# Output and down projections of a two-layer trunk with tokens as the stationary operand, and layer norms with tokens on partitions

## The chip, the cores and the metric

The kernel runs on one NeuronCore of a Trainium2 chip. The metric is the device time of one execution in microseconds, median of three runs. One execution is also profiled; its trace gives the start, duration and releaser of each instruction on TensorE (PE, with its weight loads as PEld), VectorE (DVE), ScalarE (ACT), GpSimd (POOL) and the DMA queues (SP's and ACT's among them).

## The reference

256 latent tokens `x` and 256 context tokens `ctx`, 1024 channels, pass through two layers. In layer 0 both go through all of it (512 tokens); in layer 1, the last, only the latent tokens go past the keys and values (256 tokens). All is float32. In each layer, for each stream:

```python
m = gates[..., 0, :] * attn_o + gates[..., 1, :] * conv_o + gates[..., 2, :] * pool_o
mix = m @ w_out + b_out                                          # 1024 x 1024
x = layer_norm(DEEPNORM_ALPHA * x + ml[..., 2, :] * mix, ln1_g[l], ln1_b[l])
h = modulate(x, ml[..., 3, :], ml[..., 4, :])                    # h*(1+scale)+shift
a, u = jnp.split(h @ w_up, 2, axis=-1)                           # 1024 x 5632
a = depthwise_conv(a, dw_w, dw_b)                                # 3 taps over tokens
f = (jax.nn.silu(a) * u) @ w_down                                # 2816 x 1024
x = layer_norm(DEEPNORM_ALPHA * x + ml[..., 5, :] * f, ln2_g[l], ln2_b[l])
```

`ml[..., i, :]` are six rows of 1024 numbers per layer and stream, made from a condition vector by `silu(c) @ w_ada + b_ada`. Rows 2 and 5 multiply (gate) the output and down projections.

## The kernel before

**Products.** Every fp32 matrix is held as a sum hi + lo of two fp32r parts, and a product is three passes, hi·hi, hi·lo, lo·hi (`mm3`, L389 to L395). Most products have a 128x128 piece of the weights as stationary operand and up to 512 tokens as moving operand, so the result in PSUM has channels on the partitions and tokens along the row. The q, k and v products are the other way round (`natural`): tokens stationary, 512 weight columns moving.

**Weights.** They come in as items in one fixed order (`ORDER`, made by `weight_order`). SP loads each item (`load_to`) eight items ahead, through a queue worked in order; ACT makes hi (L277), DVE makes lo by subtraction (L281), three items ahead (`split_to`), and `take` hands them out. Items named ada are products of their own for the condition rows (L329) that PE does at set places; adt and pre are side work. Activations, residuals and rows live in 55 slots of 512 floats per partition (`S`). PSUM has four buffers for products (`mmb`, names mm), three for transposes and attention (`aux`, names ax), one for ada.

**Output projection and norm 1 (L1027 to L1071).** The residual x of layer 0 is loaded by ACT's queue with channels on the partitions (L1017) and gets ALPHA and the gated bias on ACT (L1031). For each of eight 128-channel blocks, `mmB` makes the product, and `Residual.feed` evicts it on DVE (L511): product times gate, a number per channel, plus residual, into sT. In layer 0 the last four blocks are done for the two halves of the tokens (s = 0, 1) one after the other, with 256 tokens moving. After every second block `Norm.feed` transposes sT on PE (L460) to have tokens on partitions, ACT copies the result to nat (L462), and DVE takes its statistics (L467). `Norm.norm` works out mean and 1/sqrt(variance) (DVE, and a power on POOL, L475) and scales nat, on DVE (L488) and ACT (L484) by turns. `back` transposes nat back (L499), and `modulated` makes from it the input of the next products: hh on ACT (L531), h and hl on DVE (L533, L536), and xr, the residual times ALPHA and the norm's gain and offset, on ACT (L540).

**Up (L1077 to L1102).** Three up products begin by the k that are ready (`mm_by_k`). Each pair of products j is evicted by the three-tap conv, one ACT and two DVE operations (L1081, L1085, L1088), a silu on ACT and a product on DVE (L1093), and split into ah and al. A product waits until one of the four PSUM buffers is evicted.

**Down and norm 2 (L1104 to L1145).** As for the output projection, with 22 k-pieces per block in three weight items; in layer 0 the eighth block goes by halves. In layer 0 the norm leads to layer 1's first (conv) products, and the second half's norm is done later, among these. In layer 1 all products move 256 tokens, and the norm ends the kernel: gain and offset are applied on the back-transposed tiles, on ACT (L1141) and DVE (L1142), and four DMAs write the output, channels on the partitions.

**Order.** A scheduler places each engine's instructions; within an engine they run in that order. Splits (`pin`) keep the order in which they are written.

Of the kernel before, what the change touches and what calls it, by code (L numbers as in the profile page):

```python
# [13 lines left out]
P = 128  # L14
DEPTH = 2
# [24 lines left out]
NSLOT = 55  # L40
NFF = 3
# [7 lines left out]
GRP = 3  # L49
TAPS_LATER = 60  # L50
# [34 lines left out]
def weight_order(l):  # L85
# [57 lines left out]
def trunk(ctx: ExitStack, tc: tile.TileContext, xT, cT, crow, wst, vec, brow, grow, rope, icnt, ident, out):  # L143
# [140 lines left out]
    def take(it):  # L284

        while True:
# [4 lines left out]
            if ORDER[i][0] not in ("ada", "adt", "pre") and unfinished:  # L291
                unfinished.pop(0)()
# [7 lines left out]
    def take_ada():  # L300
# [10 lines left out]
        while unfinished:  # L311
            unfinished.pop(0)()
# [6 lines left out]
    ada_ps = {}  # L319
    unfinished = []  # L320
    due = []

    def ada(l, m, k):
        w = raw.pop(("ada", l, m, k))
        if k == 0:
            ada_ps[l, m] = pad.tile([P, 256], F32, tag="ad", name=uid("ad"))
        ps = ada_ps[l, m]
# [4 lines left out]
        if k == KT - 1:  # L332
            del ada_ps[l, m]
            row = sm(256, "adarow", bufs=1)
            V.tensor_copy(row, ps)
            unfinished.append(lambda: ada_end(l, m, row))
# [165 lines left out]
    class Residual:  # L502


        def __init__(self, gmod, xres, ns):
            self.ln, self.gmod, self.xres, self.ns, self.sT = Norm(), gmod, xres, ns, {}

        def feed(self, c, ps, s):
            if c not in self.sT:
                self.sT[c] = ST(self.ns * SEQ, name="sT")  # L510
            V.scalar_tensor_tensor(  # L511
                self.sT[c][:, half(s)], ps[:, half(s)], self.gmod[:, c, s:s + 1], self.xres[c][:, half(s)],
                op0=ALU.mult, op1=ALU.add,
            )
            if c % 2:
                self.ln.feed(c // 2, s, (self.sT[c - 1], self.sT[c]))

        def norm(self, s):
            self.ln.norm(s)

        def modulated(self, s, sA, sB, ag, ab, hs, xs, T, TX):

            for i in range(4):
                a = self.ln.back(i, s)
                for c2 in range(2):
# [11 lines left out]
                    if s * SEQ < TX:  # L537
                        if c not in xs:
                            xs[c] = ST(TX, name="xr")
                        A.activation(xs[c][:, half(s)], src, AF.Identity, scale=ag[:, c:c + 1], bias=ab[:, c:c + 1])  # L540

    def affine(l, name, shift, scale, tag):
# [7 lines left out]
        ag = const.tile([P, KT], F32, name=f"ag{tag}")  # L550
        ab = const.tile([P, KT], F32, name=f"ab{tag}")
        V.tensor_scalar(ag, col(l, name + "_g", 0, 8), ALPHA, None, op0=ALU.mult)
        V.tensor_scalar(ab, col(l, name + "_b", 0, 8), ALPHA, None, op0=ALU.mult)
        return sA, sB, ag, ab
# [93 lines left out]
    for l in range(DEPTH):  # L648
# [360 lines left out]
        if l == 0:  # L1009
            xres = []  # L1010
        its = [(take(("pw", l, c)), mmb()) for c in range(GRP)]
        mm_by_k(its, cT_, range(KT), T)
        for c in range(8):
            ps = its[c][1] if c < GRP else mmB(take(("pw", l, c)), cT_, T)
            if l == 0:
                xres.append(S(name="x"))
                A.dma_start(xres[c], xT[c])  # L1017
# [236 lines left out]
```

## Time and profile before

| | us |
|---|---|
| three runs | 1439.53, 1439.96, 1442.31 |
| median | 1439.96 |
| the profiled execution, its own time | 1439.88 |
| its span, first to last instruction | 1438.1 |

The span is what the trace covers. The execution's own time is 1.8 us longer. The granted clock of PE over the span was 0.993. In the rows of the profile a line with "xN" groups N instructions; the duration of a matmul reaches past the start of the next, since matmuls are pipelined, so what one costs in a stream is the distance from start to start. What stands in square brackets is the idle time ahead of an instruction and the instruction that ended it.

### The profile page before, as it was taken

How to read it: one execution, taken by the hardware profiler on the slowest of the kernel's cores; microseconds unless marked ns; L12 is line 12 of the kernel's file. 1: busy time of each engine (PE TensorE's matmuls, PEld its weight loads, DVE VectorE, ACT ScalarE, POOL GpSimd, SP SyncE). 2: the span in 40 equal slices, each digit the busy share in tenths (PEclk: the TensorE clock that was granted, in tenths of full speed). 3: DMA queues.
4: the chain of work that ended last, by engine and by line, in shares of the span. 5: the costliest groups of instructions: out<-in, count | busy, mean ns of one | idle time of the engine just before them, and what ended most of it. 6: DMA issues, size and time to landing. Idle time of an engine off the chain costs nothing.

```text
span 1438.1 us, 22130 instructions
## 1 busy us (share of the span) xinstructions
PE 1400.5 (97%) x8538; PEld 1207.9 (84%) x8538; DVE 1056.9 (73%) x1941; ACT 728.1 (51%) x1190; POOL 64.4 (4%) x59
## 2 busy tenths in 40 slices
PE   7999899999999999999999999899999999899997
PEld 5777678888877888888888888799889999799997
DVE  3598896996994747767666786379899967776653
ACT  3332346654737526554544321373687774655542
POOL 0020320000000000000000000001400000000000
PEclk9999999999999999999999999999999999999998
DMA  9654322223233415577765766878733355655540
GB/s 359 240 180 139 118 96 88 82 93 106 85 128 125 157 42 205 181 268 253 242 242 208 267 218 207 288 289 320 250 114 110 120 167 191 241 184 185 168 147 30
DMA packets 76649, 256.37 MB, mean 178 GB/s; under 512 B 8704, under 2 KB 9856, under 8 KB 76416
## 3 DMA queue, kind: packets, MB, share of 16 engines
q1 hardware_dynamic: 74416, 251.99, 50.5%
q10 hardware_dynamic: 2128, 2.96, 0.7%
q8 instruction: 67, 1.10, 0.3%
q14 instruction: 38, 0.31, 0.1%
HBM read 239.19 MB, written 15.73 MB: 177 GB/s over the span
## 4 chain that ended last, share of the span: by engine, by line
PE 73%; issue 20%; DVE 3%; ACT 2%; POOL 2%; DMA 1%; SPq 0%; POOLq 0%; ACTq 0%
PE mm L393 21%; PE mm L394 21%; PE mm L395 20%; PE ax L427 3%; PE ax L891 1%; PE ad L329 1%; PE ax L460 1%; PE ax L499 1%; POOL gc L721 1%; PE ax L393 1%; DVE lo L281 1%; PE ax L395 1%; PE ax L394 1%; PE ad L571 1%; DMA rt<-in_rope 1%
## 5 line engine op out<-in xcount | busy, mean ns | idle before, releaser
L277 ACT ACTIVATE hi<-raw 128x1024 fp32r<-128x1024 f32 (+2 forms) x212 | 218.5, 1038 | 281.5 <-PE mm L394 206.6
L393 PE MATMUL mm<-hh,hi 128*128 128x256 f32 (+1 forms) x1112 | 346.7, 317 | 8.1 <-ACT hh L531 4.6
L394 PE MATMUL mm<-hl,hi 128*128 128x256 f32 (+1 forms) x1112 | 350.3, 316 | 1.2 <-DVE hl L536 1.1
L395 PE MATMUL mm<-hh,lo 128*128 128x256 f32 (+1 forms) x1112 | 349.5, 316 | 0.0
L281 DVE TENSOR_TENSOR lo<-raw,hi 128x1024 fp32r<-128x1024 f32 (+1 forms) x193 | 229.9, 1194 | 100.6 <-ACT hi L277 96.7
L680 DVE SCALAR_TENSOR_TENSOR H<-gl,vt,H 128x502 f32<-128x502 f32 (+29 forms) x480 | 264.5, 606 | 0.1
L393 PEld LDWEIGHTS mm<-hh,hi 128*128 128x128 f32 x1112 | 209.5, 191 | 23.4 <-ACT hh L531 5.1
L394 PEld LDWEIGHTS mm<-hl,hi 128*128 128x128 f32 x1112 | 212.0, 191 | 16.8 <-DVE hl L536 2.3
L395 PEld LDWEIGHTS mm<-hh,lo 128*128 128x128 f32 x1112 | 212.1, 191 | 13.9 <-issue 1.1
L393 PE MATMUL mm<-hi,hi 128*128 128x512 f32 x464 | 186.1, 401 | 0.0
L395 PE MATMUL mm<-hi,lo 128*128 128x512 f32 x368 | 144.5, 393 | 1.1 <-DVE lo L281 1.1
L394 PE MATMUL mm<-xlo,hi 128*128 128x512 f32 x368 | 144.1, 392 | 0.0
L277 ACT ACTIVATE hi<-rawt 128x1024 fp32r<-128x1024 f32 (+2 forms) x83 | 84.9, 1025 | 114.0 <-PE mm L394 60.3
L393 PE MATMUL mm<-ah,hi 128*128 128x256 f32 (+1 forms) x374 | 123.2, 329 | 0.0
L395 PE MATMUL mm<-ah,lo 128*128 128x256 f32 (+1 forms) x374 | 122.8, 328 | 0.0
L394 PE MATMUL mm<-al,hi 128*128 128x256 f32 (+1 forms) x374 | 122.3, 327 | 0.0
L281 DVE TENSOR_TENSOR lo<-rawt,hi 128x1024 fp32r<-128x1024 f32 (+2 forms) x74 | 86.9, 1177 | 34.4 <-ACT hi L277 34.2
L393 PEld LDWEIGHTS mm<-hi,hi 128*128 128x128 f32 x464 | 87.8, 189 | 25.0 <-issue 5.7
L395 PEld LDWEIGHTS mm<-hi,lo 128*128 128x128 f32 x368 | 69.1, 188 | 16.4 <-DVE lo L281 1.9
L394 PEld LDWEIGHTS mm<-xlo,hi 128*128 128x128 f32 x368 | 69.2, 188 | 13.9 <-issue 0.4
L395 PEld LDWEIGHTS mm<-ah,lo 128*128 128x128 f32 x374 | 71.1, 190 | 6.1
L394 PEld LDWEIGHTS mm<-al,hi 128*128 128x128 f32 x374 | 71.1, 190 | 5.9
(203 smaller groups left out, 2275.9 us busy)
## 6 DMA issues: line engine op xcount, KB each, us to landing
raw<-in_wst SPq DMA_DIRECT2D x226, 512.0 KB, 4.3
rawt<-in_wst SPq DMA_DIRECT2D x154, 512.0 KB, 4.3
scr<-rawt SPq DMA_DIRECT2D x28, 512.0 KB, 4.4
lo<-scr SPq DMA_DIRECT2D x28, 512.0 KB, 6.0
ad<-in_wst SPq DMA_DIRECT2D x32, 256.0 KB, 6.0
raw<-in_wst SPq DMA_DIRECT2D x12, 384.0 KB, 3.1
x<-in_xT SPq DMA_DIRECT2D x8, 256.0 KB, 6.3
x<-in_xT ACTq DMA_DIRECT2D x8, 256.0 KB, 2.7
```

The lines of the kernel that those rows point to most:

```text
L277: pin(A.activation(hi[:, :w], r[:, :w], AF.Copy))
L281: pin(V.tensor_tensor(lo[:, :w], r[:, :w], hi[:, :w].bitcast(F32), op=ALU.subtract))
L329: PE.matmul(ps[32 * j:32 * j + 32, :], sc[:, k, :], w[:, j * 256:(j + 1) * 256], start=(k == 0), stop=(k == KT - 1),)
L393: pin(PE.matmul(ps, lh, rh, start=(first and i == 0), stop=False))
L394: pin(PE.matmul(ps, lh, rl, start=False, stop=False))
L395: pin(PE.matmul(ps, ll, rh, start=False, stop=(last and i == n - 1)))
L427: PE.matmul(ps, x[:, a:b], y[:, c:d], start=(i == 0), stop=(i == n - 1))
L460: PE.transpose(a[:, tt * 256 + c2 * P:tt * 256 + (c2 + 1) * P], pair[c2][:, o:o + P], ID)
L499: PE.transpose(a[:, c2 * 256 + tt * P:c2 * 256 + (tt + 1) * P], self.nat[i, s][:, o:o + P], ID)
L571: pin(PE.matmul(ad0_ps[q][32 * j:32 * j + 32, :P], sc[:, k, :], w[:, j * P:(j + 1) * P], start=(k == 0), stop=(k == KT - 1),))
L680: V.scalar_tensor_tensor(h[:, :, a:b], g[:, :, a + d:b + d], col(l, "dw_w", k * 8 + j), h[:, :, a:b], op0=ALU.mult, op1=ALU.add,)
L721: G.tensor_tensor(gc[:, a, b], rt[:, b], gr[:, 2 * a + b:2 * a + b + 1, :].to_broadcast([P, 2, P]), op=ALU.mult,)
```

## The change

- The output and down projections have a 128-token tile as stationary operand and 512 weight columns as moving operand (`token_products`), so their results have tokens on the partitions. Weight items are cut to fit: in layer 0, 256 rows by 512 columns, for each half h of the columns; the four token tiles hold the four PSUM buffers. In layer 1, 128 rows by all 1024 columns, and two token tiles by two halves hold them. The last items (1 or HOLD = 3 in layer 0; 3 or 5 in layer 1) are held and finished tile by tile.
- `Residual.evict`, all on DVE: product times gate row (L540), plus residual (L541), statistics (L544). `norm` scales by DVE and ACT. There are no forward transposes and no nat copies.
- The gate is now a row along the free dimension, the same for all partitions. ada results of rows 2 and 5 get their bias on DVE, go to DRAM, and come back as four (layer 1: two) tiles of 256 KB, each a row repeated on 128 partitions. Rows of b_out and of the norms' gains and offsets are loaded the same way (`param_row`). All are loads on SP.
- The residual x of layer 0 is loaded by SP with tokens on partitions.
- The residual times ALPHA and gain, plus offset, is made by `scaled`, two DVE operations for each 128 x 512 tile (L595, L596), where ACT made xr.
- In layer 0 both halves' norms of the down projection are done before the conv products of layer 1; the two back-transposes stay apart.
- At the end the gain and offset are applied on DVE along the row and the output is written token by token, with no transposes.
- An ada result that is still transposed is finished three takes later instead of one.

```diff
@@ weight_order
-    o += [("wout", l, c) for c in range(8)]
+    o += [("wout", 0, h, p) for h in range(2) for p in range(4)] if l == 0 else [("wout", 1, k) for k in range(KT)]
...
+    if l == 0:
+        down = [("down", 0, h, p) for h in range(2) for p in range(FT // 2)]
+        o += _spread(down[:-HOLD - 2], adt["down"]) + down[-HOLD - 2:]
+    else:
+        o += [("down", 1, k) for k in range(FT)]
@@ ada
+            if (l, m) in GATES:
+                V.tensor_tensor(row, ps, bias_of.pop((l, m))[:, :256], op=ALU.add)
+                gate_row[l, m] = dp.tile([2, D], F32, name=uid("grow"))
+                for s in range(1 if l else 2):
+                    load(gate_row[l, m][s:s + 1, :].rearrange("o (j x) -> (o j) x", j=4),
+                        row.rearrange("(j q) x -> j q x", q=32)[:, s, :], False)
@@ Residual
+        def evict(self, tt, h, ps):
+            t, x = S(name="tg"), self.res[tt][h]
+            V.tensor_tensor(t, ps, self.gates[tt // 2][h], op=ALU.mult)
+            V.tensor_tensor(x, t, x, op=ALU.add)
...
+            V.bn_stats(self.stats[tt][:, h, :], x)
...
-                    if s * SEQ < TX:
-                        if c not in xs:
-                            xs[c] = ST(TX, name="xr")
-                        A.activation(xs[c][:, half(s)], src, AF.Identity, scale=ag[:, c:c + 1], bias=ab[:, c:c + 1])
+        def scaled(self, tts, g, b):
+            for tt in tts:
+                for h in range(2):
+                    x = self.res[tt][h]
+                    V.scalar_tensor_tensor(x, x, ALPHA, g[h], op0=ALU.mult, op1=ALU.mult)
+                    V.tensor_tensor(x, x, b[h], op=ALU.add)
@@ token_products, layer 0
+            for h in range(2):
+                pss = [mmb() for _ in range(4)]
+                its = [(kind, 0, h, p) for p in range(nk // 2)]
+                n = len(its) - (HOLD if h else 1)
+                for p in range(n):
+                    w = take(its[p])
+                    for tt in range(4):
+                        for x in range(2):
+                            mm(pss[tt], 2 * p + x, tt, w, x * 512)
+                    run_due(2)
+                ws = [take(it) for it in its[n:]]
+                for tt in range(4):
+                    for p, w in zip(range(n, len(its)), ws):
+                        for x in range(2):
+                            mm(pss[tt], 2 * p + x, tt, w, x * 512)
+                    r.evict(tt, h, pss[tt])
+                    if h:
+                        r.norm(tt)
@@ after the first up products
-        xres = [xs[k] for k in range(KT)]
+        g, b = param_row(l, 1), param_row(l, 2)
+        for h in range(2):
+            V.tensor_scalar(b[h], b[h], ALPHA, None, op0=ALU.mult)
+        r.scaled(range(nt), g, b)
@@ the end
+            def finish(tt):
+                mv, rs = r.moments(tt)
+                for h in range(2):
+                    t, o = S(name="tg"), S(name="o")
+                    V.scalar_tensor_tensor(t, xres[tt][h], mv[:, 0:1], g[h], op0=ALU.subtract, op1=ALU.mult)
+                    V.scalar_tensor_tensor(o, t, rs, b[h], op0=ALU.mult, op1=ALU.add)
+                    (SP, A)[h].dma_start(out[tt * P:(tt + 1) * P, h * 512:(h + 1) * 512], o)
```

How the instructions move is seen in the order on each engine. First DVE in layer 0, from the output projection's norm into up, before the change: hl is the low part of up's input (the last of the second half), lo a weight split, acc with mm the conv of an up product.

```order
L536 TENSOR_TENSOR hl_5129<-h_5355,hh_5128 128x256
L533 TENSOR_SCALAR h_5369<-ax_5363,sAm_4604,sBm_4605 128x256
L536 TENSOR_TENSOR hl_5149<-h_5369,hh_5148 128x256
L281 TENSOR_TENSOR lo_5180<-raw_5177,hi_5179 128x1024
L1085 SCALAR_TENSOR_TENSOR acc_5452<-mm_5229,vt_82,acc_5452 128x2x255
L281 TENSOR_TENSOR lo_5465<-raw_5210,hi_5464 128x1024
L1088 SCALAR_TENSOR_TENSOR acc_5452<-mm_5229,vt_82,acc_5452 128x2x255
```

The same place after the change, the end of it; x are the residual's tiles, prow the rows of gain and offset. The rows ahead of these, back to the last hl, are of the same kinds (three L595, two scalings of offset rows, a lo, three L596, one L595).

```order
L595 SCALAR_TENSOR_TENSOR x_4413<-x_4413,prow_5247 128x512
L596 TENSOR_TENSOR x_4373<-x_4373,prow_5253 128x512
L596 TENSOR_TENSOR x_4413<-x_4413,prow_5251 128x512
L595 SCALAR_TENSOR_TENSOR x_4453<-x_4453,prow_5249 128x512
L595 SCALAR_TENSOR_TENSOR x_4501<-x_4501,prow_5247 128x512
L596 TENSOR_TENSOR x_4453<-x_4453,prow_5253 128x512
L596 TENSOR_TENSOR x_4501<-x_4501,prow_5251 128x512
L595 SCALAR_TENSOR_TENSOR x_4541<-x_4541,prow_5249 128x512
L1186 SCALAR_TENSOR_TENSOR acc_5276<-mm_5052,vt_82,acc_5276 128x2x255
L596 TENSOR_TENSOR x_4541<-x_4541,prow_5253 128x512
L1189 SCALAR_TENSOR_TENSOR acc_5276<-mm_5052,vt_82,acc_5276 128x2x255
```

The sixteen operations of `scaled` have come between the last hl and the two conv operations of the first up product.

Next PE in layer 0's output projection, second half of the tokens, before: mhi and mlo are the token parts, hi and lo the weight's.

```order
L394 MATMUL mm_4814<-mlo_4325,hi_4650 128x256
L460 MATMUL ax_4931<-ID,sT_4929 128x128
L460 MATMUL ax_4931<-ID,sT_4903 128x128
L460 MATMUL ax_4931<-ID,sT_4929 128x128
L395 MATMUL mm_4814<-mhi_4323,lo_4651 128x256
L393 MATMUL mm_4814<-mhi_4332,hi_4650 128x256
```

And after, where the projection's last matmuls meet the back-transposes of the first half.

```order
L423 MATMUL mm_4737<-hi_4740,mhi_4546 128x512
L424 MATMUL mm_4737<-lo_4741,mhi_4546 128x512
L425 MATMUL mm_4737<-hi_4740,mlo_4548 128x512
L568 MATMUL ax_4914<-ID,x_4309 128x128
L568 MATMUL ax_4914<-ID,x_4327 128x128
L568 MATMUL ax_4930<-ID,x_4309 128x128
```

The 256-column matmuls and the transposes of sT are gone; matmuls of 512 columns run up to the back-transposes, which read the residual's own tiles.

Last SP's queue at the start of up in layer 0, after: adarow is the gate row's ada result, grow its copy in DRAM, raw the weights of items to come.

```order
L212 DMA raw_5035<-in_wst 128x1024
L212 DMA raw_5286<-in_wst 128x1024
L212 DMA grow_5049<-adarow_5047 4x256 x2
L212 DMA raw_5329<-in_wst 128x1024
L212 DMA prow_5247<-in_rows 128x512
L212 DMA prow_5249<-in_rows 128x512
L212 DMA prow_5251<-in_rows 128x512
L212 DMA prow_5253<-in_rows 128x512
L212 DMA raw_5362<-in_wst 128x1024
```

The gate row's write and four row loads have come between weight loads.

More of the change, by code (lines that the diff above doesn't have):

```diff
@@ L40 @@
 NSLOT = 55
+HOLD = 3
 NFF = 3
@@ L502, in trunk @@
     class Residual:
[L505 to L516, printed above, removed]
@@ new lines, in moments, with norm @@
+        def moments(self, tt):
+            mv = sm(2, "mv")
+            V.bn_aggr(mv, self.stats[tt][:, 0:2, :].rearrange("p a b -> p (a b)"))
+            ve, rs = sm(1, "ve"), sm(1, "lrs")
+            V.tensor_scalar(ve, mv[:, 1:2], LN_EPS, None, op0=ALU.add)
+            G.tensor_tensor(rs, ve, mhalf[:, :1], op=ALU.pow)
+            return mv, rs
+        def norm(self, tt):
+            mv, rs = self.moments(tt)
+            nm = sm(1, "nm")
+            V.scalar_tensor_tensor(nm, mv[:, 0:1], -1.0, rs, op0=ALU.mult, op1=ALU.mult)
+            a, b = self.res[tt]
+            V.tensor_scalar(a, a, mv[:, 0:1], rs, op0=ALU.subtract, op1=ALU.mult)
+            A.activation(b, b, AF.Identity, scale=rs, bias=nm)
@@ L549, in affine, with gate_tiles @@
         V.tensor_tensor(sA, sA, bc2(col(l, name + "_g", 0, 8)), op=ALU.mult)
[L550 to L554, printed above, removed]
+        return sA, sB
+    def gate_tiles(l, m):
+        return [row_tiles(gate_row[l, m][s:s + 1, :], "gate") for s in range(1 if l else 2)]
@@ new lines, in token_products, with mm @@
+    def token_products(l, kind, src, r, between, after):
+        nk = len(src)
+        def mm(ps, k, tt, w, o):
+            mm3(ps, [(part(src[k], tt * P, (tt + 1) * P), part(w, o, o + 512))], first=(k == 0), last=(k == nk - 1))
+        if l == 0:
+            for h in range(2):
[16 more added lines that the diff above has]
+                        r.norm(tt)
+                        if tt == 1:
+                            between()
+        else:
+            pss = [[mmb() for _ in range(2)] for _ in range(2)]
+            its = [(kind, 1, k) for k in range(nk)]
+            n = nk - (HOLD if kind == "wout" else NW)
+            for k in range(n):
+                w = take(its[k])
+                for tt in range(2):
+                    for h in range(2):
+                        mm(pss[tt][h], k, tt, w, h * 512)
+            ws = [take(it) for it in its[n:]]
+            for tt in range(2):
+                for h in range(2):
+                    for k, w in zip(range(n, nk), ws):
+                        mm(pss[tt][h], k, tt, w, h * 512)
+                    r.evict(tt, h, pss[tt][h])
+                after(tt)
```

177 lines of the change are left out of this document (94 added, 83 removed).

## Prediction

> **What bounds the kernel now.** The page's first parts come first: the engines' shares and the chain of work that ended last, by engine.
>
> ```profile
> span 1438.1 us, 22130 instructions
> PE 1400.5 (97%) x8538; PEld 1207.9 (84%) x8538; DVE 1056.9 (73%) x1941; ACT 728.1 (51%) x1190; POOL 64.4 (4%) x59
> PE 73%; issue 20%; DVE 3%; ACT 2%; POOL 2%; DMA 1%; SPq 0%; POOLq 0%; ACTq 0%
> ```
>
> PE is busy all but 3% of the span. So a microsecond of PE work removed counts wherever PE runs solid, and the question is only where it will begin to wait. The second view is the table by stretches of time over the stages that the change touches: output projection and down projection of layer 0, the same two of layer 1, and the tail (start:end, length, busy time of PE, PEld, DVE, ACT, POOL, granted clock, DMA share, GB/s).
>
> ```profile
> 499.00:548.00 49.00, 48.60 (x319) 44.00 (x318) 24.02 (x47) 14.41 (x21) 0.69 (x1) 1.00 0.17 57
> 798.70:924.60 125.90, 125.90 (x638) 105.50 (x638) 83.23 (x139) 32.84 (x39) 0.70 (x1) 1.00 0.72 249
> 1196.40:1221.20 24.80, 24.80 (x207) 24.27 (x206) 15.81 (x26) 9.60 (x11) 0.00 (x0) 1.00 0.54 184
> 1360.90:1425.50 64.60, 64.60 (x539) 64.22 (x537) 28.55 (x35) 21.70 (x25) 0.00 (x0) 1.00 0.30 97
> 1425.50:1438.10 12.60, 4.49 (x20) 3.42 (x19) 5.34 (x15) 4.82 (x9) 0.70 (x1) 0.61 0.25 83
> ```
>
> Four stretches are PE alone, and the last, 12.6 us, is the chain of the final norm with PE mostly idle. The profiled execution took 1439.88 us, 1.8 more than its span and 0.1 under the median 1439.96; I subtract from 1439.9. About 0.2% of it, 2.9 us, is what a measurement of this kernel can tell from no change.
>
> **The products.** From the timeline of PE (start, duration, line, shapes), the first and the last row of ten matmuls of 512 columns, of nine of 256, of fourteen of the q projection, which already has tokens stationary and 512 weight columns moving, and a row of eight transposes:
>
> ```profile
> 499.65 0.39 PE L393 MATMUL mm<-mhi,hi 128*128 128x512 f32 x1
> 501.92 0.39 PE L394 MATMUL mm<-mlo,hi 128*128 128x512 f32 x1
> ...
> 525.02 0.28 PE L394 MATMUL mm<-mlo,hi 128*128 128x256 f32 x1
> 526.10 0.28 PE L394 MATMUL mm<-mlo,hi 128*128 128x256 f32 x1
> ...
> 999.66 0.39 PE L393 MATMUL mm<-hi,hh 128*128 128x512 f32 x1
> 1002.84 0.39 PE L395 MATMUL mm<-hi,hl 128*128 128x512 f32 x1
> ...
> 929.03 1.04 PE L499 MATMUL ax<-ID,nat 128*128 128x128 f32 x8
> ```
>
> Start to start, 512 columns take 2.27/10 = 0.227 us whichever operand moves (3.18/14), 256 columns 1.08/9 = 0.120. Two of 256 become one of 512, so a pair saves 0.013 us. Layer 1 has only 256 tokens, and half of layer 0's output projection and an eighth of its down projection ran by halves: 96 + 66 + 96 + 264 = 522 pairs, 6.8 us. A transpose takes (1.04 - 0.28)/7 = 0.11 us. The forward ones (L460 of sT: 32, 32, 16, 16) go, and the last 16 back. The back ones of the other three norms stay.
>
> Stage by stage this is: output projection, layer 0, 192 x 0.2265 = 43.5 us for 49.0, -5.5. Down projection, layer 0, 528 x 0.2265 = 119.6 for 125.9, -6.3. Down projection, layer 1, 264 x 0.2265 = 59.8 for 64.6, -4.8. Output projection, layer 1, 96 x 0.2265 = 21.7, and I add 0.6 of waiting: the gate and bias rows of layer 1 are put together on DVE between two weight splits (8 operations of about 0.6 us); 22.3 for 24.8, -2.5. These four, -19.1, are the firm part, each good to 1 us.
>
> [...]
>
> **Start of up, layer 0.** This is what the change makes worse. The scaled residual (xr, L540) was 24 evictions on ACT. Now it is `scaled` on DVE: in layer 0 eight STT and eight TT of 512 columns, which the order puts behind the last hl and ahead of the conv of the first up product. The fifth up product waits for the second conv operation (L1088, now L1189), which frees its PSUM buffer; there are four. DVE and PE before, from the last hl of the second half; then layer 1's, where PE waits at this very place; then xr's row:
>
> ```profile
> 572.39 0.42 DVE L536 TENSOR_TENSOR hl<-h,hh 128x256 fp32r<-128x256 f32 x1
> 576.46 1.23 DVE L281 TENSOR_TENSOR lo<-raw,hi 128x1024 fp32r<-128x1024 f32 x1 [3.64 <-ACT hi L277]
> 577.60 0.74 DVE L1085 SCALAR_TENSOR_TENSOR acc<-mm,vt,acc 128x510 f32<-128x510 f32 x1
> 579.39 0.74 DVE L1088 SCALAR_TENSOR_TENSOR acc<-mm,vt,acc 128x510 f32<-128x510 f32 x1
> 580.05 0.74 DVE L1085 SCALAR_TENSOR_TENSOR acc<-mm,vt,acc 128x510 f32<-128x510 f32 x1
> ...
> 584.23 0.68 DVE L1100 TENSOR_TENSOR al<-acc,ah 128x512 fp32r<-128x512 f32 x1
> 584.83 0.68 DVE L1093 TENSOR_TENSOR acc<-acc,mm 128x512 f32<-128x512 f32 x1
> ...
> 576.00 0.40 PE L394 MATMUL mm<-hl,hi 128*128 128x512 f32 x1
> ...
> 1238.99 0.42 DVE L536 TENSOR_TENSOR hl<-h,hh 128x256 fp32r<-128x256 f32 x1
> 1245.15 0.36 PE L393 MATMUL mm<-hh,hi 128*128 128x256 f32 x1 [1.55 <-DVE acc L1088]
> ...
> L540 ACT ACTIVATE xr<-ax,abm,agm 128x256 f32<-128x256 f32 x24 | 13.3, 566 | 5.0 <-DVE h L533 4.9
> ```
>
> Before, the fourth product (24 matmuls of 512 columns, the first recorded at 576.00) ends near 581.1, 33.1 after the projection's end at 548.0, and L1088 has ended at 580.13: PE doesn't wait. Now count from the projection's new end W. Without the last forward transposes, copies and half-width statistics PE could start the fifth product at W + 30.7 by my count (2.4 sooner: the gaps and 12 transposes of this stretch). DVE ends its last hl at W + 23.4 (before: 24.8). Behind that stand 8 STT x 0.66 (579.39 to 580.05) + 8 TT x 0.60 (584.23 to 584.83) + two scalings of 512 columns, 0.45 each by estimate + one lo at 1.14 (576.46 to 577.60) + two conv operations x 0.66 = 13.4, so the buffer comes free at W + 36.9 and PE waits 6.2 us. With -2.4 this is +3.8. Behind it I take DVE to catch up, a product being 5.4 us of PE. If hl ends 3 us earlier or later the wait is 3 or 9 us.
>
> A wait of that length also costs clock. At the conv start PE waited 3.60 us, and then, by the table of stretches, ran at this clock:
>
> ```profile
> 931.62 1.06 ACT L277 ACTIVATE hi<-raw 128x1024 fp32r<-128x1024 f32 x1 [4.81 <-DMA raw<-in_wst]
> 933.66 1.22 PE L393 MATMUL mm<-hh,hi 128*128 128x256 f32 x4 [3.60 <-ACT hh L531]
> ...
> 933.00:937.00 4.00, 3.33 (x17) 3.34 (x18) 2.91 (x11) 2.50 (x6) 0.70 (x1) 0.57 0.94 352
> ...
> 951.82 0.39 PE L393 MATMUL mm<-hh,hi 128*128 128x256 f32 x1 [1.91 <-ACT sg L702]
> ```
>
> Some 3 us at 0.57 lose 1.3 to 1.5 us of solid matmuls. I take +1.5 here, for a total of +5.3 (range 0 to +9).
>
> [...]
>
> **Start of up, layer 1.** The norm's chain is about as long as before, but two weight splits (2 x 1.14) stand ahead of the first h: the last hl comes 19.6 us after the projection's end for 18.2, +1.4. Before, 5.7 us passed from there to L1088's end, 2.44 of them idle. Now four STT, four TT, two scalings, one lo and two half-width conv operations take 2.6 + 2.4 + 0.9 + 1.1 + 0.8 = 7.9, +2.2. The buffer was the bound already, so both count, and with 0.7 for the clock this is +4.3 (range 0 to +8).
>
> **Start of layer 1's convolution products.** The first must wait for hh on ACT. Two weight splits, whose raw tiles come in after the first ada matmuls, stand ahead of hh on ACT, as the row at 931.62 shows for before: the first product comes 9.5 us after the down projection, for 9.0, and the gain is not here. The wait at 951.82 is for GLU evictions that the second half's statistics and nat copies had held back; that norm is now done ahead. I take it as gone, with some xr and gb evictions, together -3.3 (range -5 to +1).
>
> **Tail.** The rows of the last norm, with those that price the new one:
>
> ```profile
> 1425.53 0.48 DVE L511 SCALAR_TENSOR_TENSOR sT<-mm,mod,xr 128x256 f32<-128x256 f32 x1 [7.44 <-PE mm L395]
> 1428.63 0.70 POOL L475 TENSOR_TENSOR lrs<-ve,mhalf 128x2 f32<-128x2 f32 x1 [203.20 <-DVE ve L474]
> 1430.00 3.84 PE L499 MATMUL ax<-ID,nat 128*128 128x128 f32 x16 [3.37 <-DVE nat L488]
> 1434.47 0.54 DVE L1142 TENSOR_SCALAR o<-ax,vt 128x256 f32<-128x256 f32 x1 [0.46 <-ACT o L1141]
> 1435.04 0.40 ACTq L1143 DMA_DIRECT2D out_x<-o  x1
> ...
> L904 DVE TENSOR_TENSOR m<-ax,g 128x512 f32<-128x512 f32 x8 | 5.5, 682 | 0.5 <-PE ax L427 0.5
> L467 DVE BATCH_NORM_STATS2 bst<-ax 128x6 f32<-128x256 f32 x72 | 26.9, 421 | 16.0 <-ACT nat L462 16.0
> ```
>
> Now: 0.2 to the eviction, TT 0.7, the dependent TT 0.78, bn_stats of 512 columns 0.75 by estimate from 0.42 for 256, bn_aggr 0.3, ve 0.17, POOL with its two hand-overs 0.95 (the first STT of the output lies beside it), then STT, STT, STT 2.0: 5.9 us, and the output's 3.06 from issue to the end (1435.04 to 1438.1): 8.9 for 12.6, -3.7 (range -5 to -2).
>
> **Edits costed at nothing.** 256 KB row loads (gates, rows, bias rows) and xn join SP's queue, ahead of weight loads. Output projection, layer 0, moves 57 GB/s, so the eight x loads and six rows (3.5 MB) are covered; at the 352 GB/s quoted above they would be 10 us without cover. At layer 0's down projection the gate rows wait for slots that the last up product frees, with four down items (24 matmuls, 5.4 us each) loaded ahead of them: 21.7 us of cover for a landing of some microseconds. A gate row is written to DRAM a stage before it is read.
>
> **The sum.** -19.1 + 5.3 + 4.3 - 3.3 - 3.7 = -16.5: 1423.4 us.
>
> **The rivals.**
> (1) `scaled` does not hold PE: DVE is further ahead than I count, or it stalls elsewhere. For it: DVE stood idle 3.64 us there before. Against it: layer 1's wait at 1245.15 shows no slack. Without its share of the waits and clock losses, 6.2 + 1.5 and 2.2 + 0.7, it is 1423.4 - 10.6 = 1412.8. Chance 0.2.
> (2) The waits grow by half or more at both up starts, or the conv start too gives back its gain: up to +9 and +8 in place of 5.3 and 4.3, +1 in place of -3.3, sum -4.8 at the worst, 1435, and some 1430 midway. Chance 0.17.
> (3) Slower. `scaled` begins with an STT that needs a parameter row, and DVE takes its work in order, the buffer's release behind it. On SP that row is queued behind the write of the gate row (which waits for adarow on DVE) and seven to ten weight loads of 512 KB, which wait for ada matmuls. At the 352 GB/s of the stretch above ten loads take 15 us, and the order shows this at both up starts. Each microsecond that the row lands after the last hl then counts in full, since the block is behind it: over 8.3 us at both starts the 16.5 are spent, and at 10 us it is 1423.4 + 20 = 1443. Against it: the ada matmuls start with the projection's end, some 20 us ahead of the last hl. Chance 0.06.
> (4) It is without effect on time: the shorter stages are given back as waits one for one, within 2.9 us. The chance is 0.02: the order shows the transposes gone and the halves merged, and PE was full there.
>
> **How the numbers follow.** The forecast has 0.55, and I name 1423. Its own range is 1417 to 1430. To hold 8 in 10 it is taken from 1411, with most of rival 1, to 1432, with over half of rival 2. Faster is 0.55 + 0.2 + 0.17 = 0.92; same 0.03, rival 4 and the milder sixth of rival 3; slower the rest of it, 0.05.
>
> **What would show it.** Right: the four stages at 43.5, 119.6, 22 and 59.8 us; a PE wait of 3 to 9 us released by DVE acc L1189 at the fifth up product of layer 0, 4 to 6 in layer 1, with a clock under 1 behind; no wait for sg in the conv stage near 950; a tail near 9. Wrong: 512-column matmuls not at 0.227 with tokens stationary; no wait for L1189; or a first STT of `scaled` that waits for a DMA for microseconds.

## The result, and the profile after

The changed kernel took 1432.92 us (median of four runs, 1432.51 to 1435.02) where the kernel before took 1440.72 (four runs, 1439.53 to 1442.31): a ratio of 0.9948, 95% interval 0.9931 to 0.9965. It is faster by 7.8 us. The forecast was 16.9 us to 1423, with a range that ended at 1432. Its sign was right and the time lies outside the range. The profiled execution took 1433.0 us, 6.9 less than the one of before; the spans differ by the same 6.9.

The page's first parts, of after:

```profile
span 1431.2 us, 20768 instructions
PE 1382.7 (97%) x7896; PEld 1173.4 (82%) x7896; DVE 1093.3 (76%) x1931; ACT 683.0 (48%) x1088; POOL 66.1 (5%) x65
PE 88%; DVE 7%; DMA 2%; ACT 1%; issue 1%; POOL 1%; SPq 0%; POOLq 0%; DVEq 0%; ACTq 0%
```

PE has 17.8 us less to do, about as much as the firm part of the forecast (19.1), but the span fell by 6.9: 10.9 us of waits came in. The chain of waits names the engines: DVE had 3% of it and has 7%, DMA 1% and now 2%.

The table by stretches finds the places. Columns as in the prediction. First the stretches of before between the stages that it quoted (layer 0's norm and up; layer 1 up to its last conv projection; layer 1's norm and up), then all of after in the order of time, from layer 0's output projection on.

```profile
548.00:798.80 250.80, 250.46 (x1231) 207.98 (x1229) 175.18 (x233) 131.15 (x171) 0.69 (x1) 1.00 0.65 227
924.60:1172.20 247.60, 239.28 (x1697) 217.80 (x1696) 218.38 (x531) 167.71 (x305) 24.58 (x22) 0.99 0.59 208
1221.10:1360.40 139.30, 134.63 (x1143) 131.24 (x1142) 99.40 (x160) 80.70 (x130) 0.69 (x1) 1.00 0.57 194
```

```profile
496.50:539.90 43.40, 43.40 (x194) 35.97 (x193) 33.35 (x55) 9.57 (x10) 1.99 (x3) 1.00 0.25 86
540.10:798.90 258.80, 251.85 (x1225) 208.66 (x1224) 185.40 (x248) 122.79 (x153) 0.82 (x2) 0.99 0.65 228
798.90:918.60 119.70, 119.70 (x529) 98.88 (x527) 85.86 (x133) 28.23 (x29) 1.62 (x3) 1.00 0.74 259
918.80:1167.50 248.70, 241.20 (x1701) 219.68 (x1700) 217.67 (x519) 159.81 (x286) 21.86 (x22) 0.98 0.60 212
1191.50:1214.50 23.00, 22.15 (x98) 17.69 (x96) 20.71 (x31) 7.63 (x8) 0.00 (x0) 1.00 0.79 266
1214.70:1360.90 146.20, 138.68 (x1138) 135.56 (x1138) 107.72 (x170) 76.09 (x119) 1.48 (x2) 0.95 0.59 200
1360.90:1420.90 60.00, 60.00 (x265) 49.28 (x264) 31.32 (x35) 19.82 (x20) 0.98 (x1) 1.00 0.36 125
1420.90:1431.20 10.30, 0.20 (x1) 0.00 (x0) 6.49 (x11) 0.00 (x0) 0.89 (x1) 0.77 0.20 76
```

| stretch | before | after | change | forecast |
|---|---|---|---|---|
| output projection, layer 0 | 49.0 | 43.4 | -5.6 | -5.5 |
| norm and up, layer 0 | 250.8 | 258.8 | +8.0 | +5.3 |
| down projection, layer 0 | 125.9 | 119.7 | -6.2 | -6.3 |
| layer 1 to its conv projection | 247.6 | 248.7 | +1.1 | -3.3 |
| output projection, layer 1 | 24.8 | 23.0 | -1.8 | -2.5 |
| norm and up, layer 1 | 139.3 | 146.2 | +6.9 | +4.3 |
| down projection, layer 1 | 64.6 | 60.0 | -4.6 | -4.8 |
| tail | 12.6 | 10.3 | -2.3 | -3.7 |

These add to -4.5. The rest, -2.4, lies ahead of layer 0's output projection, which starts at 496.5 for 499.0; the ten variants below start it between 495.3 and 497.8. Its main term stands where the first gate's ada result is made (PE's waits and the stretch with its clock, before and after):

```profile
173.92 0.69 PE L374 MATMUL ax<-ID,adarow 128*128 128x128 f32 x2 [4.04 <-DVE adarow L335]
172.00:179.00 7.00, 5.08 (x14) 4.08 (x14) 6.25 (x13) 2.79 (x14) 3.13 (x3) 0.51 0.39 112
...
172.08 0.50 PE L423 MATMUL mm<-hi,hi 128*128 128x512 f32 x1 [1.40 <-DVE nat L915]
174.37 0.50 PE L423 MATMUL mm<-hi,hi 128*128 128x512 f32 x1 [0.63 <-DVE nat L915]
172.00:179.00 7.00, 6.29 (x26) 4.92 (x27) 7.00 (x15) 4.47 (x19) 3.88 (x4) 1.00 0.34 107
```

Before, PE transposed this result; it waited 4.04 us for DVE's copy of it and ran at half clock (0.51) behind. A gate row is no longer transposed, so PE waits 1.40 and 0.63 us there, at a clock of 1.00. The last matmul ahead of this place starts 0.8 us later than before (170.29 for 169.48), the next transposes 2.2 us sooner (202.05 for 204.26). The forecast has no term for this.

The four projections came as forecast, -18.2 for -19.1. The loss is in the three starts behind a norm, and a little in the tail. Each has its rows.

Layer 0's start of up (timeline of DVE, then PE). The last hl ends at 564.6:

```profile
564.18 0.43 DVE L588 TENSOR_TENSOR hl<-h,hh 128x256 fp32r<-128x256 f32 x1
566.43 1.90 DVE L595 SCALAR_TENSOR_TENSOR x<-x,prow 128x512 f32<-128x512 f32 x3 [1.82 <-DMA prow<-in_rows]
577.27 0.74 DVE L1186 SCALAR_TENSOR_TENSOR acc<-mm,vt,acc 128x510 f32<-128x510 f32 x1
578.53 0.74 DVE L1189 SCALAR_TENSOR_TENSOR acc<-mm,vt,acc 128x510 f32<-128x510 f32 x1
579.42 0.76 PE L423 MATMUL mm<-hh,hi 128*128 128x512 f32 x1 [6.41 <-DVE acc L1189]
```

From the first `scaled` operation to the end of L1189 it is 12.8 us (forecast 13.4), and PE waits 6.41 us for it (6.2). Ahead of the block DVE waited 1.82 us for a parameter row.

Layer 1's conv start, with the row of the chain of waits for the DMA that ends it:

```profile
928.52 1.23 PE L423 MATMUL mm<-hh,hi 128*128 128x256 f32 x4 [4.52 <-ACT hh L583]
932.38 0.42 DVE L356 TENSOR_TENSOR adarow<-ad,bg 128x256 f32<-128x256 f32 x1 [2.16 <-DMA bg<-in_bgate]
933.20 0.58 PE L424 MATMUL mm<-hl,hi 128*128 128x256 f32 x1 [0.92 <-DVE hl L588]
...
923.59 8.77 DMA bg<-in_bgate
```

The bias row of layer 1's gate (128 KB) was issued behind weight loads, landed 8.77 us later, and DVE stopped at adarow, with the next hl behind it.

Layer 1's start of up, PE and DVE:

```profile
1222.01 2.18 PE L568 MATMUL ax<-ID,x 128*128 128x128 f32 x9 [2.22 <-DVE x L559]
1244.10 0.36 PE L423 MATMUL mm<-hh,hi 128*128 128x256 f32 x1 [3.41 <-DVE acc L1189]
...
1218.11 0.67 DVE L540 TENSOR_TENSOR tg<-mm,gate 128x512 f32<-128x512 f32 x1
```

The last eviction comes at 1218.11, 3.4 us after the projection's last matmul; the wait for L1189 was 1.55 and is 3.41 us.

And the clock, in four stretches behind these waits:

```profile
579.40:583.40 4.00, 3.98 (x10) 3.16 (x11) 4.00 (x6) 1.23 (x2) 0.00 (x0) 0.51 0.39 130
928.50:938.50 10.00, 9.06 (x40) 8.66 (x41) 6.93 (x16) 3.63 (x7) 0.00 (x0) 0.51 0.93 356
1218.00:1232.00 14.00, 9.90 (x53) 8.49 (x50) 11.37 (x24) 6.34 (x11) 0.55 (x1) 0.63 0.99 363
1244.00:1250.00 6.00, 5.90 (x37) 5.93 (x38) 4.80 (x7) 2.57 (x5) 0.00 (x0) 0.72 0.54 175
```

PE ran at half speed for 4, 10, some 10 and 3 us. Before it did so for 3 us in all of this (0.57 in 933 to 937); at 1225 to 1239, the start of up in layer 1, its clock was 1.00.

### The profile page after: what moved, and what is told of

It is laid out like the page before. It is cut to its first block, busy times and chain, and to the rows that moved or that the text cites. A ratio compares the mean times of both kernels' runs of the same rounds, so it can differ in the third digit from the quotient of the medians.

```text
span 1431.2 us, 20768 instructions
## 1 busy us (share of the span) xinstructions
PE 1382.7 (97%) x7896; PEld 1173.4 (82%) x7896; DVE 1093.3 (76%) x1931; ACT 683.0 (48%) x1088; POOL 66.1 (5%) x65
## 4 chain that ended last, share of the span: by engine, by line
PE 88%; DVE 7%; DMA 2%; ACT 1%; issue 1%; POOL 1%; SPq 0%; POOLq 0%; DVEq 0%; ACTq 0%
PE mm L423 26%; PE mm L424 26%; PE mm L425 26%; PE ax L457 3%; DVE lo L283 1%; PE ax L991 1%; PE ad L349 1%; DVE H L780 1%; DMA prow<-in_rows 1%; PE ax L425 1%; PE ax L423 1%; PE ad L671 1%; PE ax L424 1%; DMA bg<-in_bgate 1%; DVE x L596 1%
## 5 line engine op out<-in xcount | busy, mean ns | idle before, releaser
L423 PE MATMUL mm<-hh,hi 128*128 128x256 f32 (+1 forms) x1112 | 354.6, 321 | 14.9 <-DVE acc L1189 9.8
L279 ACT ACTIVATE hi<-raw 128x1024 fp32r<-128x1024 f32 x208 | 215.8, 1046 | 309.4 <-PE mm L424 124.3
L423 PEld LDWEIGHTS mm<-hh,hi 128*128 128x128 f32 x1112 | 215.1, 194 | 30.7 <-issue 12.0
L279 ACT ACTIVATE hi<-rawt 128x1024 fp32r<-128x1024 f32 (+1 forms) x83 | 86.7, 1048 | 108.4 <-PE mm L425 51.4
L283 DVE TENSOR_TENSOR lo<-rawt,hi 128x1024 fp32r<-128x1024 f32 (+1 forms) x72 | 86.5, 1205 | 32.5 <-ACT hi L279 32.5
L423 PE MATMUL mm<-hi,ah 128*128 128x512 f32 x264 | 102.8, 390 | 0.0
L424 PE MATMUL mm<-lo,ah 128*128 128x512 f32 x264 | 102.8, 389 | 0.0
L425 PE MATMUL mm<-hi,al 128*128 128x512 f32 x264 | 102.6, 389 | 0.0
L381 DVE CUSTOM_DVE_ANT_0 prod<-rawt,cb,vt 128x1024 f32<-128x1024 f32 x48 | 61.5, 1282 | 4.2 <-DMA rawt<-in_wst 3.6
L423 PEld LDWEIGHTS mm<-hi,ah 128*128 128x128 f32 x264 | 49.6, 188 | 10.9 <-issue 0.3
```

Source lines behind the costliest of these rows:

```text
L279: pin(A.activation(hi[:, :w], r[:, :w], AF.Copy))
L283: pin(V.tensor_tensor(lo[:, :w], r[:, :w], hi[:, :w].bitcast(F32), op=ALU.subtract))
L381: tc.keep_in_program_order(V.tensor_tensor_reduce(prod, w, cb[:, s], 1.0, col(l, "b_ada", m * 8 + c), ALU.mult, ALU.add, mods[l, m][:, c, ...
L423: pin(PE.matmul(ps, lh, rh, start=(first and i == 0), stop=False))
L424: pin(PE.matmul(ps, lh, rl, start=False, stop=False))
L425: pin(PE.matmul(ps, ll, rh, start=False, stop=(last and i == n - 1)))
```

## The experiments

Theory 1 from here on: the block of `scaled` operations costs what was counted, rows that land late behind weights cost as much again, and what PE waits costs clock behind it. Its rivals are named with each run. Times are given as ratios to runs of the kernel before on the same chip, with their 95% interval; the changed kernel's is 0.9948.

**e1_spread.** `scaled`'s two operations per tile go into the loop over the up products.

```diff
-        r.scaled(range(nt), g, b)
+        put_off = [(tt, h) for tt in range(nt) for h in range(2)]
...
             act[j] = (hi, lo)
             run_due(2)
+            if j >= 2 and put_off:
+                tt, h = put_off.pop(0)
+                x = xres[tt][h]
+                V.scalar_tensor_tensor(x, x, ALPHA, g[h], op0=ALU.mult, op1=ALU.mult)
+                V.tensor_tensor(x, x, b[h], op=ALU.add)
```

> The scaled residual is made inside the loop over the up products, a 128x512 tile per j, where the changed kernel makes all of it between the last hl and the first conv operation; nothing else moves. Theory 1 (the block on VectorE costs what it looks like): the waits of 6.6 us (layer 0) and 3.6 us (layer 1) for the conv operation at the fifth up product go to under 1 us, with the slow clock of 2 and 1.5 us behind them: 12 to 13 us, about 1420. Rival (the rows that come late are what held VectorE, the block only follows them): three of the operations still stand ahead of the conv operation and wait for the rows, so most of the wait stays and the gain is under 4 us, 1429 or more.

0.9860 (0.9844 to 0.9877), 1421.56 us, near what was expected. Norm and up of layer 0, and of layer 1:

```profile
541.40:791.80 250.40, 249.85 (x1225) 207.36 (x1224) 184.70 (x248) 122.26 (x153) 0.84 (x2) 1.00 0.69 236
1209.80:1352.00 142.20, 135.56 (x1138) 132.60 (x1138) 107.40 (x170) 76.29 (x119) 1.49 (x2) 0.98 0.62 206
```

In layer 0 the wait is gone and 8.4 us with it, all that was lost there; in layer 1 4.0. So the block's place is a cause, and the rows alone are not. The conv start is no better than in the changed kernel (250.0 for 248.7).

**e2_rows_ahead.** Rows a stage earlier: layer 0's norm rows with its gate rows, layer 1's ahead of the conv projection, bias rows ahead of the stage that uses them.

```diff
         mT = []
+        bias_ahead(l, 5)
         if l == 0:
             xres = [[], [], [], []]
+        else:
+            gates, ob, g0, b0 = gate_tiles(l, 2), param_row(l, 0), param_row(0, 3), param_row(0, 4)
+            g, b = param_row(l, 1), param_row(l, 2)
...
         if l == 0:
             gates, ob = gate_tiles(l, 2), param_row(l, 0)
+            g, b = param_row(l, 1), param_row(l, 2)
...
             hs = {}
+            bias_ahead(1, 2)
```

> Parameter rows and bias rows are loaded a stage earlier (layer 0: with the gate rows ahead of the output projection; layer 1: ahead of the last conv projection's products; the bias row of layer 1's gate ahead of the down projection), so that no VectorE operation waits for a row queued behind weights. The block of scaled operations stays where it is. Theory 1: the 1.8 us row wait goes in layer 0, the 2.2 us bias wait at layer 1's conv start, and in layer 1's output projection the 7.5 us wait whose backlog makes the last eviction 3.5 us late: 5 to 9 us in all, 1424 to 1428, while the waits for the conv operation stay at about 5 and 3.5 us. Rival (the late rows have cover, only the block counts): within 2 us of 1433.

0.9885 (0.9869 to 0.9900), 1423.60 us, but not in the way expected: the block didn't stay where it was. With its rows there, the scheduler slipped six of the eight tiles between the h's of the first half, so the wait for L1189 vanished in layer 0 and smaller ones came (1.45 and 0.65 us for hl, 1.49 us for an ada weight). In layer 1's conv projection PE now waited:

```profile
1176.72 0.57 PE L426 MATMUL mm<-ch,hi 128*128 128x256 f32 x1 [3.82 <-DVE pwo L1126]
```

The row products of layer 1 (L1146, L1147) and four weight splits stood ahead of pwo, which frees a PSUM buffer; the projection took 29.6 us for 24.0. So the run mixes three effects and tells little by its time. The conv start improved by 3.3 (245.4 for 248.7; see e7).

**e3_keep_clock.** Matmuls of the identity that nobody reads fill PE's waits.

```diff
+    def warmed(n):
+        a = aux()
+        for _ in range(n):
+            tc.keep_in_program_order(PE.matmul(a[:, :P], ID, ID, start=True, stop=True))
...
+            if j == 2:
+                warmed(56 if l == 0 else 30)
             pa = upps.get((j, 0)) or mmB(take(("up", l, j, 0)), hT2, T)
...
             take_ada()
+            warmed(24)
             r.modulated(0, *aff, hs, T)
...
             take_ada()
+            warmed(40)
             r.modulated(0, *aff, hs, NTOK)
```

> Matmuls of the identity that nobody reads are added where the changed kernel's TensorE waits: 56 ahead of the fifth up product of layer 0, 30 ahead of layer 1's, 24 after the ada products of layer 1, 40 after those at layer 1's conv start. Each takes 0.11 us, so they fit into waits of 6.6, 3.6, 2.5 and 4.7 us. Theory 1 (a wait costs clock behind it, and the changed kernel lost 7 us more of it than the kernel before): the clock stays at 1.00 behind the first two waits and the time falls by 4 to 8 us, 1425 to 1429. Rival (the low clock lies beside waits anyway): no gain, or 1 to 2 us slower by the added matmuls.

0.9984 (0.9974 to 0.9993), 1438.45 us: slower than the changed kernel. The cause is a wrong size. The row of these matmuls counts 300 for 150 in the program (the x150 at its end counts every second record):

```profile
L611 PE MATMUL ax<-ID x300: 270/275/377, 573.1 to 1249.2; 128*128 128x128 f32 x150
```

Each float32 product ran as two, 0.225 us, and 34 us of them overfilled waits of 17.

**e4_spread_rows.** e1 and e2 together.

> Both: scaled operations inside the up loop and rows loaded a stage earlier. Theory 1: the two gains add but for the row waits that the first already hides, 16 to 20 us off 1433, 1413 to 1417. If the waits are one chain (block behind row), the sum is no better than the better of the two alone, about 1420.

0.9882 (0.9868 to 0.9897), 1423.54 us: no better than either, as the second case has it, yet not as one chain. Stage by stage the gains are there (conv start 243.4), and so are e2's two losses: conv projection 30.6 us for 24.0, and norm and up of layer 0 253.4 us, 3.0 more than in e1, since rows that are there early let the scheduler put `scaled` between the h's.

**e5_keep_clock_half.** e3 with 27, 15, 10 and 19 matmuls.

```diff
-                warmed(56 if l == 0 else 30)
+                warmed(27 if l == 0 else 15)
...
-            warmed(24)
+            warmed(10)
...
-            warmed(40)
+            warmed(19)
```

> The run with added identity matmuls again, with half their number (27, 15, 10, 19), since each took 0.225 us and not 0.11, and they overfilled the waits. They now take 6.1, 3.4, 2.3 and 4.3 us, inside waits of 6.6, 3.6, 2.5 and 4.7. Theory 1: where TensorE does not fall idle, the clock behind stays at 1.00, which gives back 1.7 us at layer 0's up, 2.5 to 3.5 at layer 1's conv start, 2 to 4 at layer 1's up: 1425 to 1428. Rival (the low clock costs nothing, TensorE would wait anyway for what comes next): 1432 to 1434.

0.9905 (0.9885 to 0.9926), 1427.79 us. The same stretches, and the wait:

```profile
576.00:584.00 8.00, 7.79 (x45) 6.66 (x45) 8.00 (x11) 1.96 (x4) 0.00 (x0) 1.00 0.33 115
928.00:940.00 12.00, 9.61 (x80) 9.53 (x80) 6.30 (x14) 4.69 (x7) 0.00 (x0) 1.00 0.70 237
578.42 0.47 PE L423 MATMUL mm<-hh,hi 128*128 128x512 f32 x1 [0.21 <-DVE acc L1197]
```

The clock stays at 1.00 (in 1206 to 1250, layer 1's start of up, too), and matmuls that do nothing made the kernel faster: norm and up of layer 0 by 2.0 us (256.8), conv start 2.2 (246.5), norm and up of layer 1 2.8 (143.4). So the clock behind the waits cost 7 us. The prediction had 2.2 on top of the 1.3 to 1.5 that before lost at the conv start.

**e7_bias_ahead.** Of e2 only the bias rows.

```diff
         mT = []
+        bias_ahead(l, 5)
...
             hs = {}
+            bias_ahead(1, 2)
```

> Only the bias rows for the gates are loaded a stage earlier. Theory 1: the 2.2 us wait of the gate's ada result on VectorE at layer 1's conv start goes, with the second wait of TensorE there (1.2 us) and part of the slow clock: 2 to 4 us, 1429 to 1431. Rival (conv start is bound by the weights alone, whose splits on ScalarE end at the same time): 0 to 1 us.

0.9909 (0.9887 to 0.9930), 1427.77 us, more than the 2 to 4 us that were expected. adarow at the conv start no longer waits for a DMA:

```profile
922.06 0.42 DVE L359 TENSOR_TENSOR adarow<-ad,bg 128x256 f32<-128x256 f32 x1 [0.21 <-PE ad L352]
917.70:1163.10 245.40, 239.96 (x1701) 217.59 (x1700) 218.57 (x519) 159.56 (x286) 21.71 (x22) 0.99 0.61 214
1210.00:1353.00 143.00, 135.93 (x1137) 133.19 (x1137) 107.56 (x170) 76.02 (x119) 1.48 (x2) 0.98 0.62 204
```

Conv start -3.3, and layer 1's up -3.2. But at the conv start the order on ACT moved too. First the changed kernel's first hh, behind two weight splits; then this run's, ahead of them, and its clock from the first product on:

```profile
927.92 0.55 ACT L583 ACTIVATE hh<-ax,sBn,sAn 128x256 fp32r<-128x256 f32 x1
...
922.62 0.56 ACT L586 ACTIVATE hh<-ax,sBn,sAn 128x256 fp32r<-128x256 f32 x1 [0.38 <-PE ax L571]
923.20:933.20 10.00, 8.33 (x55) 7.80 (x54) 6.60 (x14) 5.51 (x9) 0.00 (x0) 0.83 1.01 404
```

PE's first product starts 5.5 us after the down projection for 9.7, and PE runs at half clock for some 3 us for 10 (0.83 and 0.51 over ten microseconds). All five runs with the bias rows ahead (e2, e4, e6, e7, e9) have this order and no other run has it, so how much of the 3.3 is the row's landing and how much the order, no run separates. At layer 1's up no wait for the row shows in the changed kernel; what shows is where adarow stood, among the hl's or ahead of all of them, and the clock of the 19 us from the first up matmuls on. First the changed kernel's two rows, then this one's:

```profile
1227.36 0.42 DVE L356 TENSOR_TENSOR adarow<-ad,bg 128x256 f32<-128x256 f32 x1
```

```profile
1224.00:1243.00 19.00, 15.44 (x101) 14.75 (x100) 15.62 (x31) 9.12 (x15) 0.00 (x0) 0.79 0.73 251
```

```profile
1215.46 0.41 DVE L359 TENSOR_TENSOR adarow<-ad,bg 128x256 f32<-128x256 f32 x1
```

```profile
1219.30:1238.00 18.70, 14.69 (x115) 14.22 (x114) 16.86 (x34) 9.21 (x15) 0.00 (x0) 0.96 0.67 250
```

How much of the 3.2 is that one operation and how much the weight splits that moved with it, no run separates.

**e8_rows1_ahead.** Layer 1's gate, b_out and ln2 rows loaded in the attention part, two loads at a time.

```diff
+            if l and n in (10, 11, 12, 13):
+                early.append(gate_tiles(l, 2) if n == 10 else param_row(*((l, 0), (0, 3), (0, 4))[n - 11]))
...
-            g, b = param_row(0, 3), param_row(0, 4)
+            gates, ob, g, b = early
```

> Only the gate, b_out and ln2 rows of layer 1's output projection are loaded earlier, in the attention part. Theory 1 (the backlog of VectorE in the output projection makes its last eviction 3.5 us late, and the norm and up start after it): from the projection's start to the down projection's 4 to 6 us less than the 169.4 of the changed kernel, 1427 to 1429. Rival (the norm's chain and the ada products set that start, the backlog is caught up): under 1.5 us.

0.9947 (0.9930 to 0.9964), 1433.61 us: nothing. The projection is shorter (21.6 us), its up hardly (145.6), and the conv projection gives it back (28.6 us for 24.0): the row work now stands ahead of its splits on DVE,

```profile
1171.59 0.58 PE L424 MATMUL mm<-clo,hi 128*128 128x256 f32 x1 [2.25 <-DVE clo L434]
```

with a slow clock behind (0.50 in 1172 to 1176, 0.67 in 1176 to 1178). By this run the late eviction of 1218.11 doesn't set layer 1's start of up; e6 qualifies that.

**e6_pinned_spread.** e1 with each tile held behind the conv operation of its j by a dependency without a semaphore (its lines stand under e9), e7's bias rows, and e8's rows.

> Scaled operations held behind the conv operation of product j (j = 2 on) by a dependency without a semaphore, so that they can neither stand ahead of it nor slip between the h's; bias rows a stage earlier; the gate, b_out and ln2 rows of layer 1's output projection loaded in the attention part, where DMA has room, and not in one burst ahead of the conv projection. Theory 1: all three gains and none of the two losses of the run with both (h's delayed in layer 0, 5.6 us of weight loads late in layer 1's conv projection): layer 0's up 8 us, conv start 3, layer 1 6 us under the changed kernel, 1413 to 1417. If the up start of layer 1 or the conv start has another bound, 1418 to 1421.

0.9816 (0.9793 to 0.9839), 1414.10 us. The time is as expected. One reason in the expectation is not: it puts e2's loss in the conv projection down to weight loads, and e2's own row shows DVE's pwo. Nor are all losses gone. The conv projection takes 27.5 us for 24.0, with row work ahead of its splits as in e8, and layer 1's up takes 139.1, as before the change (139.3), at a full clock:

```profile
1152.50:1180.00 27.50, 26.24 (x196) 25.95 (x197) 19.62 (x38) 16.39 (x29) 0.00 (x0) 0.88 0.40 128
1201.80:1340.90 139.10, 133.34 (x1137) 130.49 (x1137) 106.28 (x168) 76.11 (x119) 1.06 (x2) 1.00 0.63 209
```

**e9_spread_bias.** e6 without e8's rows.

```diff
-                V.scalar_tensor_tensor(x, x, ALPHA, g[h], op0=ALU.mult, op1=ALU.mult)
+                i = V.scalar_tensor_tensor(x, x, ALPHA, g[h], op0=ALU.mult, op1=ALU.mult)
+                tc.add_manual_dep(
+                    i.ins, conv.ins.name, mybir.DependencyInfo(mybir.DependencyClass.NoSync, mybir.DependencyReason.DATA),
+                    reason="after the conv",
+                )
```

> Scaled operations pinned behind the conv operations of the up loop, and bias rows a stage earlier; layer 1's other rows stay where the changed kernel has them, since loading them earlier won 7 us in layer 1's projection and up and lost 3.5 us in its conv projection. Theory 1 (bias rows and block are the two causes, the rows of layer 1's output projection are not): layer 0's up 250.5, conv start to conv projection 243 to 244, conv projection 24.0, output projection 22.7, up 140 to 141: 1411 to 1414. Rival (the rows of layer 1 count as well): 1416 to 1420.

0.9803 (0.9787 to 0.9819), 1414.40 us where the kernel before took 1442.80: the lowest ratio here, not told apart from e6's, and just above the 1411 to 1414 expected (up 141.9 for 140 to 141).

```profile
538.90:789.40 250.50, 249.83 (x1225) 207.38 (x1224) 185.75 (x248) 123.06 (x153) 0.78 (x2) 1.00 0.68 235
909.30:1152.90 243.60, 238.21 (x1701) 216.07 (x1700) 218.16 (x519) 159.51 (x286) 22.88 (x22) 1.00 0.61 215
1200.10:1342.00 141.90, 137.01 (x1137) 134.22 (x1137) 107.29 (x170) 76.12 (x119) 1.48 (x2) 0.96 0.61 205
```

Against the changed kernel -8.3, -5.1 and -4.3. Two edits, the place of 24 operations on DVE and the time of three small loads (with the order that came with it), give back about 20 us. Layer 1's up is 2.8 us longer than in e6, with a clock of 0.96 for 1.00. The two kernels differ in e8's rows alone, so these cost 2.8 us there when they are late, and 3.5 us in the conv projection when they are early.

**e10_rows0_block.** Layer 0's norm rows ahead, the block held between the last hl and the first conv operation by dependencies.

```diff
+            ahead2 = param_row(l, 1), param_row(l, 2)
...
-        r.scaled(range(nt), g, b)
+        held = r.scaled(range(nt), g, b, last_hl[0] if l == 0 else None)
...
+            if j == 0 and l == 0:
+                tc.add_manual_dep(conv.ins, held.ins.name, mybir.DependencyInfo(mybir.DependencyClass.NoSync, mybir.DependencyReason.DATA), reason="order")
```

> Only layer 0: the rows of the norm's gain and offset are loaded ahead of its output projection, and the block of scaled operations is held between the last hl and the first conv operation. Theory 1 (block and late row are links of one chain, 13 us and 1.8 us): the wait at the fifth up product falls from 6.6 to about 4.8 us, the slow clock behind it stays, 1430 to 1432. Rival (the row alone holds the block, whose operations would else end before TensorE comes): the wait is under 1 us, 1424 to 1426.

0.9921 (0.9900 to 0.9942), 1430.82 us, as expected.

```profile
577.62 0.76 PE L423 MATMUL mm<-hh,hi 128*128 128x512 f32 x1 [4.96 <-DVE acc L1197]
```

The wait falls by 1.45 us from 6.41: the late row's share. The rest is the block. The stage gets only 0.7 us shorter (258.1), since the half clock behind the wait (0.50 in 578 to 582, 0.75 in 582 to 584) lasts 5.4 us for 3.9.

## Why the prediction was wrong

- **The products** were right. 43.4, 119.7, 23.0 and 60.0 us against 43.5, 119.6, 22.3 and 59.8. After the change too 512 columns took 0.2265 us whichever operand is stationary.
- **Start of up, layer 0**: the block was right to 0.6 us (12.8 for 13.4; its two scalings, for which the 0.45 each had no row, took 0.34 each). PE's wait was right in size (6.4 for 6.2) by luck: PE was ready 32.7 us after the projection and not 30.7, and the buffer came free at 39.1 and not 36.9, by an hl 1.1 us late and a row 1.8 us late. Without the late row the wait is 4.96 (e10). Wrong was the -2.4 ahead of it. The last matmul of the three first up products came 27.6 us after the projection's last one, where it was 28.2: 0.6 sooner. The stretch has 32 transposes for 38, and I had counted 12 as gone. Of the remaining 0.9, 0.4 is clock (1.9, from 4 us at 0.51, for 1.5).
- **Edits costed at nothing** is one step that failed. The bias rows of the gates were not priced at all: I had them among rows "covered", by DMA's mean load in another stage. At layer 1's conv start nine loads of 512 KB were issued in the 7.6 us ahead of the row, it landed 8.77 us after its issue, and DVE waited 2.16 us for it and PE 0.92. With the bias rows ahead (e7) the stage is 3.3 us shorter, layer 1's up 3.2, and the whole 5.6 (0.0039 of 1441; each of the two ratios is uncertain by 2.5 to 3 us). That is an upper bound for the rows, since the orders on ACT and DVE moved with them, and it overlaps the clock's price. This is rival 3's mechanism, in another row, at a milder size; the row that rival 3 named cost 1.45 us of wait in layer 0 (e10). The gate's transposes, which the change drops, were costed at nothing too: that is most of the -2.4 at the start, a gain by luck.
- **The clock** is the other step that failed: a right mechanism, and a term far too small. It was priced at 2.2 us for two waits, and at nothing at the conv start. It took 7 (e5); less the 1.3 to 1.5 of the kernel before that is, by estimate, some 5.6. The 0.7 of it in layer 1 was an estimate that no row of before shows; behind the waits there the clock was 0.63 in 1218 to 1232 and 0.72 in 1244 to 1250. How long the slow clock lasted differed from place to place: behind the single wait at 579 it was 4 us at 0.51; at the conv start, where a second wait ended 4.7 us after the first, 10 us at 0.51; in e7, with shorter waits there, some 3 us (0.83 over ten).
- **Start of layer 1's convolution products**: -3.3 forecast, +1.1 found. The wait for sg at 951.82 did go, and the first product came 9.7 us after the down projection (9.5 forecast). What came in is the 0.92 us behind adarow and the 10 us of half clock (0.51) for 3; how the rest divides is open. The stage is -2.2 in e7, and with a full clock (1.00 over the stage) -4.0 in e9, but in both the first product comes 4 us sooner by the order on ACT, which no forecast had. So it isn't shown that the gain was there and was spent on the late row.
- **Tail**: 10.3 for 8.9. The last eviction began on DVE 1.0 us late, behind the first tile's output, which I had left out of the queue.

In sum: +2.7 at layer 0's up, +4.4 at the conv start, +2.6 and 0.7 in layer 1, +1.4 in the tail, 0.2 in other projections, less the 2.4 at the start: +9.6 on -16.5. The time came out as rival 2's worst case, 1435, less the 2.4, but by half of its mechanism: the conv start gave back its gain, while the waits for L1189 hardly grew (6.41 and 3.41 for 6.2 and some 3.7). What stays open is how the late bias row and the order on ACT share the conv start.

## What to carry to other kernels

An engine that runs its queue in order makes every operation's place a price: work that nobody needs for 200 us cost 8 us here because it stood ahead of the operation that frees a PSUM buffer. A small load had no cover from the mean load of its queue (128 KB landed 8.77 us after its issue, behind nine loads of 512 KB); look at what is issued ahead of it in the last 10 us. And a wait on PE is to be priced with the slow clock behind it: here 2 us behind a single wait of 6.4, and 7 us behind the waits of three stages. A run that moves one load can let the scheduler move other work; read the order on every engine before the gain is put down to the load.

## What the hardware showed that was not expected

- Useless matmuls made this kernel faster: 71 of them in PE's waits kept the clock at 1.00 and gained 7 us in three stages (0.9905 for 0.9948), while 150 of them, twice too long for the waits, lost it again (0.9984).
- A float32 product of 128x128 ran as two matmuls, 0.225 us, in e3 and e5 (300 records for 150 in e3; 54 for 27 and 38 for 19 in e5), where a transpose of the same shape takes 0.11.
